# A decoder layer's first stage: keys stored by remainders of 16, a recurrence of one copy and eight links, and a step moved in its stream

## The chip, the cores and the metric

The kernel runs on one core of one Trainium2 chip. The metric is the device time in microseconds, median of several runs. The engines are named as in the trace: PE (matmuls; PEld its weight loads), DVE, ACT, POOL, and SP, which here only issues transfers.

## The reference

A decoder layer over 2048 tokens of 1024 features in float32. After an RMS norm, one input projection gives queries, keys and values for 8 attention heads of 64 features, and query, forget gate, input and output gate for 8 heads of a gated linear recurrence. Attention runs three times per head and the results are weighted by their softmax denominators:

```python
DILATED_CONFIGS = ((128, 1), (512, 4), (2048, 16))   # window, dilation
scores = einsum('bgnqhd,bgnkhd->bgnhqk', qb, kk) / sqrt(Dh)   # blocks of 128 queries, keys of this and the last block
scores = where(valid, scores - slope * (sub_dist * dilation), -inf)
```

With dilation d a block takes every d-th token: 128 queries, and the 128 keys of the block and those of the block before it (with dilation 16 there is only one block per remainder). The recurrence works on chunks of 32 tokens here, and on chunks of 64 in the kernel:

```python
log_f = log(lb + (1 - lb) * sigmoid(f_raw)); key = (1 - lb) * sigmoid(-f_raw); q = silu(q)
b = cumsum(log_f)                                     # within a chunk
A = where(causal, (q * exp(b)) @ (key * exp(-b)).T, 0)
dS = (key * exp(b_last - b)).T @ v;  S_next = exp(b_last) * S + dS
o = A @ v + (q * exp(b)) @ S
```

An output projection follows, then 32 experts in 4 groups, of which each token takes 2, and a last norm.

## The kernel before

**Stages.** Stage A (up to about 1134 us) computes projections, attention and recurrence for four pairs of heads. Then come output projection and router, and from about 1388 us the experts. Only stage A is changed; the later ones begin when it ends.

**Order of PE.** PE's instructions in stage A stand in an order written out by a planner (`Runner`, line 123). Work is cut in steps, each with a cost in ns and a list of steps that it follows with a delay (`Step(fn, cost, after)`). There are streams: H, the recurrence; G, weights; A, attention; F, projections. Within a stream the order is fixed; at each point the first stream whose next step is ready by the planner's clock goes on. The other engines' queues follow from that order and priorities: a step that is emitted later has, as a rule, its ACT, DVE and POOL instructions later. Each engine works its queue in order.

**Attention.** Queries and keys of a pair are held with the features on partitions, keys as high and low float16 halves (`qk_chunk`, drained from the accumulators by ACT in line 358 and by DVE in line 359). A block of scores (line 436) is four matmuls: two heads, two halves. The 128 queries are the weights that PE loads, the up to 256 keys stream past. `block_cols` takes both at steps of the dilation in tokens, 2 bytes each. After exponentials (ACT, line 453) and transposing transfers come the value matmuls (lines 471 and 473). The dilations run in the order 1, 16, 4. In the last one `combine` loads the results of the other two (tile `R`, line 506) and mixes them (POOL lines 529 and 531, DVE among them line 532).

**Recurrence.** Four token tiles of 128 make a quad, four quads a pair; each tile's projections are lines 567 to 569. Six steps follow for a quad: `gates` (lines 595 to 609, on ACT, DVE and POOL: logarithms, sigmoids, products), `decays` (line 615: sums over a chunk), `states` (line 643: the eight dS of a quad; ACT drains them in line 647; then a chain over eight chunks in which POOL scales the last state, line 658, and DVE adds dS, line 661), `turns` (transposes, line 672, drained by ACT in line 674), `within` (line 683, masked by DVE in line 684) and `outputs` (lines 693 and 697). The accumulators for these, named hg, have two buffers. The projections of quad q+2 come behind the outputs of quad q, since they share buffers.

## Time and profile before

| | us |
|---|---|
| median of 3 runs (2206.78 to 2219.48) | 2217.72 |
| the profiled execution | 2217.23 |
| its span, first to last instruction | 2215.3 |
| PE busy in the span | 1967.0 (89%) |
| DVE busy | 1493.8 (67%) |
| ACT busy | 1201.4 (54%) |
| POOL busy | 567.3 (26%) |

The mean granted clock of PE was 0.943 of full speed. The profile is of one execution; a group of instructions by line shows its busy time, the mean of one in ns, and the idle time of the engine just before them with what ended it. A name such as `hg<-Sp,qT` says which tile is written and which are read. In a timeline, `x4` is four instructions that follow one another; PE's instructions overlap, so what four cost is the distance between the start of theirs and the start of the next instruction, and not their duration.

### The profile page before, as it was taken

Reading aid. Unit: us, or ns where it says so; the run is one execution under the profiler, and the core shown is the slowest. Engines: PE = TensorE matmul, PEld = TensorE weight load, DVE = VectorE, ACT = ScalarE, POOL = GpSimd, SP = SyncE. Lnnn points to the kernel's source line nnn. Section 1 sums busy time; section 2 is a strip of 40 time slices with the busy share of each in tenths; the row PEclk is TensorE's granted clock in tenths of the full one; section 3 lists DMA queues with packets and bytes.
Section 4 is the critical chain, followed back from the end, with each engine's and each line's share of the span. In section 5 each row is a group of like instructions: output and inputs, shape, how many; then the busy total and the mean of one; then the engine's idle time right before and its main releaser. Section 6 shows DMA issues by size and latency. Waiting matters only on the chain. (4 is left out here: it accounts for less than half of the span.)

```text
span 2215.3 us, 39749 instructions
## 1 busy us (share of the span) xinstructions
PE 1967.0 (89%) x13753; PEld 1345.8 (61%) x13777; DVE 1493.8 (67%) x4121; ACT 1201.4 (54%) x2646; POOL 567.3 (26%) x620
## 2 busy tenths in 40 slices
PE   4998978999899998899888998699999999999981
PEld 4645565555655556455444445569999977766750
DVE  6657787767857777567887677756656656556525
ACT  6455653765547655566554343456556655555524
POOL 2303244123431335411431112212233222111110
PEclk9998988998999998999899998799999999999995
DMA  7333254532535324553578995799999999999857
GB/s 229 85 94 96 66 128 112 114 90 70 118 101 123 83 75 113 174 119 71 128 168 226 290 253 164 253 353 315 312 311 314 329 315 313 325 325 321 302 149 299
DMA packets 438896, 433.37 MB, mean 196 GB/s; under 512 B 242644, under 2 KB 325716, under 8 KB 438176
## 3 DMA queue, kind: packets, MB, share of 16 engines
q1 hardware_dynamic: 420464, 382.74, 56.7%
q0 software_dynamic: 14064, 46.46, 8.5%
q8 instruction: 109, 1.79, 0.3%
q10 hardware_dynamic: 4160, 1.58, 0.3%
q14 instruction: 99, 0.81, 0.1%
HBM read 305.30 MB, written 66.29 MB: 168 GB/s over the span
## 5 line engine op out<-in xcount | busy, mean ns | idle before, releaser
L1660 DVE TENSOR_TENSOR eL<-eraw,eH 128x1024 bf16<-128x1024 f32 x248 | 298.0, 1218 | 107.9 <-ACT eH L1654 97.0
L1654 ACT ACTIVATE eH<-eraw 128x1024 fp32r<-128x1024 f32 x252 | 258.4, 1053 | 123.8 <-PE acc L1745 48.8
L453 ACT ACTIVATE P<-S,orow,fqk 128x256 f32<-128x256 f32 (+1 forms) x384 | 195.0, 512 | 172.3 <-DVE orow L447 94.1
L567 PE MATMUL proj<-whh,x 128*128 128x512 f16 x512 | 202.4, 395 | 0.1
L568 PE MATMUL proj<-whl,x 128*128 128x512 f16 x512 | 200.1, 391 | 0.0
L569 PE MATMUL proj<-whh,x 128*128 128x512 f16 x512 | 199.5, 390 | 0.0
L1726 PE MATMUL acc<-xs,eH 128*128 128x352 f32 (+15 forms) x1216 | 195.2, 313 | 1.8 <-DVE xs L1704 1.8
L436 PE MATMUL S<-k,qs 128*128 128x256 f16 (+1 forms) x768 | 172.4, 355 | 13.9 <-ACT P L453 10.9
L1726 PEld LDWEIGHTS acc<-xs,eH 128*128 128x128 f32 x1216 | 176.2, 190 | 4.7 <-issue 2.2
L440 DVE CUSTOM_DVE_ANT_0 S<-S,bias 128x256 f32<-128x256 f32 (+1 forms) x384 | 141.4, 369 | 54.8 <-PE S L436 51.6
L456 DVE TENSOR_TENSOR Ps<-P,Ps 128x256 f16<-128x256 f32 (+1 forms) x192 | 129.7, 675 | 68.8 <-ACT Ps L455 67.2
L1828 POOL DMA_INDIRECT x2d<-yo,sidx x49 | 105.2, 2146 | 255.7 <-DVE yo L1803 95.8
L1776 PE MATMUL acc<-hs,eD 128*128 128x176 f32 (+15 forms) x1216 | 165.1, 295 | 4.9 <-DVE ts L1751 3.0
L1776 PEld LDWEIGHTS acc<-hs,eD 128*128 128x128 f32 x1216 | 161.1, 190 | 6.0 <-DVE ts L1751 3.9
L1687 POOL DMA_INDIRECT xg<-h2d,gidx x49 | 56.1, 1146 | 334.0 <-PE tr L1701 159.6
L436 PEld LDWEIGHTS <-qs 128*128 128x128 f16 x768 | 89.5, 123 | 69.3 <-issue 20.3
L260 POOL TENSOR_TENSOR wraw<-wraw,g 128x1024 f32<-128x1024 f32 x44 | 84.7, 1928 | 167.8 <-DMA wraw<-in_w_in_dram 134.5
L1744 PE MATMUL acc<-eH,xs 128*128 128x512 f32 x208 | 118.4, 569 | 0.0
L1788 PE MATMUL acc<-eD,hs 128*128 128x512 f32 x208 | 98.0, 609 | 21.2 <-ACT yo L1801 11.5
L386 PE MATMUL proj<-wh,x 128*128 128x128 f16 x512 | 96.5, 231 | 18.9 <-DVE V L394 18.9
L455 ACT ACTIVATE Ps<-P 128x256 f16<-128x256 f32 (+1 forms) x192 | 102.8, 536 | 7.6 <-DMA PT<-Ps 5.0
L658 POOL TENSOR_SCALAR sw<-Sp,hw 128x128 f32<-128x128 f32 x112 | 53.3, 476 | 196.5 <-DVE Sp L661 106.5
(396 smaller groups left out, 4891.6 us busy)
## 6 DMA issues: line engine op xcount, KB each, us to landing
eraw<-in_w_gate_dram SPq DMA_DIRECT2D x128, 512.0 KB, 7.1
eD<-in_w_down_dram SPq DMA_DIRECT2D x128, 512.0 KB, 6.4
eraw<-in_w_up_dram SPq DMA_DIRECT2D x124, 512.0 KB, 6.3
wraw<-in_w_in_dram SPq DMA_DIRECT2D x41, 512.0 KB, 4.1
od<-orow SPq DMA_DIRECT2D x64, 132.0 KB, 2.0
R<-od SPq DMA_DIRECT2D x64, 132.0 KB, 2.4
xt<-in_x_dram SPq DMA_DIRECT2D x16, 512.0 KB, 4.8
wraw<-in_w_out_dram SPq DMA_DIRECT2D x16, 512.0 KB, 4.1
```

What stands on the lines that cost most here:

```text
L436: nc.tensor.matmul(ps[:, h, :W], q, self.block_cols(D['k'][h][:, x], br, blk, True), start=(x == 0), stop=(x == 1))
L440: nc.vector.tensor_tensor_reduce(ps[:, h, :W], ps[:, h, :W], bias[:, 256 - W:256], 1.0, -3.0e38, OP.add, OP.max, mx[:, h:h + 1])
L453: nc.scalar.activation(P[:, h], ps[:, h, :W], AF.Exp, bias=nm[:, h:h + 1], scale=f[:, h:h + 1], accum_out=orow[:, 130 + h:131 + h])
L456: nc.vector.tensor_tensor(hv[:, 1], P, hv[:, 0], op=OP.subtract)
L567: nc.tensor.matmul(ps, self.XH[n // 4][:, k, ns], W['whh'][:, k, :], start=(k == 0), stop=False)
L568: nc.tensor.matmul(ps, self.XH[n // 4][:, k, ns], W['whl'][:, k, :], start=False, stop=False)
L569: nc.tensor.matmul(ps, self.XL[n // 4][:, k, ns], W['whh'][:, k, :], start=False, stop=(k == KT - 1))
L1654: nc.scalar.activation(H, raw, AF.Copy)
L1660: (nc.gpsimd if on_pool else nc.vector).tensor_sub(L, raw, H.bitcast(F32))
L1726: nc.tensor.matmul(gu[:, i, 0:2 * cap], w[:, o:o + 128], xs[:, k], start=(k == 0), stop=False, skip_group_check=True)
L1744: nc.tensor.matmul(gu[:, j], xs[:, k, 0], H[:, fs], start=(k == 0), stop=False)
L1776: nc.tensor.matmul(py[:, j, 0:cap], W['w_down', f][:, o:o + 128], hs[:, f], start=(f == 0), stop=(f == 3))
```

## The change

**Keys.** Each stretch of 512 tokens of the keys is stored by remainder of 16: 16 groups of 32 keys. `block_keys` then reads runs of 32 neighbouring keys for dilations 16 and 4, and runs of 8 for dilation 1. The drains read the accumulators at steps of 16 elements (64 bytes). Queries stay as they were. Since the keys of a block now come in another order, the values for dilation 1 are loaded again from memory in that order, those for dilation 4 too, and each dilation has its own table of distances, which SP loads.

**Recurrence.** dS is multiplied by the decays by POOL (two instructions), the chain is eight instructions on DVE over a compact tile `Sc`, and two ACT copies put the states in `Sp`. The transposed keys have their own tile `kT`. `R` has one buffer. States, turns and score products are split into two steps each, and their order is turns, states, products, outputs, with other costs and delays.

**Order.** The gates of a quad are put into the stream H five places from its end, which is ahead of the states (`s0`) of the quad before.

```diff
@@ -354,9 +356,13 @@
             a, b = slice(64 * h, 64 * h + 64), slice(64 - 64 * h, 128 - 64 * h)
             t = D["qk"[which]][h]
             hi, lo = (t[a, cs], t[b, cs]) if which == 0 else (t[a, 0, cs], t[a, 1, cs])
+            src = ps[a]
+            if which == 1:
+                src = src.rearrange("p (a r) -> p r a", r=16)
+                hi, lo = (x.rearrange("p (r a) -> p r a", r=16) for x in (hi, lo))
             sc = PSC / 2 if which == 0 and h == 0 else PSC
-            nc.scalar.activation(hi, ps[a], AF.Copy, scale=sc)
-            nc.vector.scalar_tensor_tensor(lo, ps[a], sc, hi, op0=OP.mult, op1=OP.subtract)
+            nc.scalar.activation(hi, src, AF.Copy, scale=sc)
+            nc.vector.scalar_tensor_tensor(lo, src, sc, hi, op0=OP.mult, op1=OP.subtract)
             if which == 1:
                 nc.gpsimd.dma_start(t[b, :, cs], t[a, :, cs])
 
@@ -389,38 +395,64 @@
...
-    def block_cols(self, t, br, blk, keys):
+    def block_queries(self, t, br, blk):
 
         dil = DIL[br]
         r, n = blk % dil, blk // dil
-        lo = n - 1 if keys and n else n
-        return t[:, r + lo * 128 * dil:r + (n + 1) * 128 * dil - dil + 1:dil]
+        return t[:, r + n * 128 * dil:r + (n + 1) * 128 * dil - dil + 1:dil]
+
+    def block_keys(self, t, br, blk):
+
+        r, n = blk % DIL[br], blk // DIL[br]
+        t = t.rearrange("p (g r a) -> p g r a", g=4, r=16)
+        if br == 3:
+            return t[:, :, r]
+        if br == 2:
+            return t.rearrange("p g (q c) a -> p c g q a", c=4)[:, r, max(n - 1, 0):n + 1]
+        cols = [t[:, m // 4, :, 8 * (m % 4):8 * (m % 4) + 8] for m in (n - 1, n) if m >= 0]
+        if len(cols) == 1:
+            return cols[0]
+        a, b = cols
+        return bass.AP(tensor=a.tensor, offset=a.offset, ap=[a.ap[0], [b.offset - a.offset, 2], *a.ap[1:]])
+
...
@@ -431,9 +463,9 @@
         f, bias = D['f'], D['bias', br]
         ps = self.psum([128, 2, 256], "S", 2)
         for h in range(2):
-            q = self.block_cols(D['q'][h], br, blk, False)
+            q = self.block_queries(D['q'][h], br, blk)
             for x in range(2):
-                nc.tensor.matmul(ps[:, h, :W], q, self.block_cols(D['k'][h][:, x], br, blk, True), start=(x == 0),
+                nc.tensor.matmul(ps[:, h, :W], q, self.block_keys(D['k'][h][:, x], br, blk), start=(x == 0),
                                  stop=(x == 1))
         mx = self.asm.tile([128, 2], F32, name="mx")
         for h in range(2):
@@ -499,7 +531,7 @@
...
-        R = self.ap_.tile([128, 2, 2, ROW], F32, name="R", bufs=2)
+        R = self.ap_.tile([128, 2, 2, ROW], F32, name="R", bufs=1)
@@ -633,55 +665,53 @@
             nc.vector.tensor_add(w, sv[:, :, 0], sv[:, :, 1])
             nc.scalar.activation(w, w, AF.Exp)
 
-        def states():
+        def states(ch):
             ek, v, w = L['sg'][:, :, 128:256], L['hq'][:, :, 384:512], L['w']
-            ds = []
-            for ch in range(2):
-                hs = slice(64 * ch, 64 * ch + 64)
-                pd = self.psum([128, 4, 128], "hg", 2)
-                for i in range(4):
-                    nc.tensor.matmul(pd[:, i, :], ek[hs, i, :], v[hs, i, :], start=True, stop=True)
-                d = hp.tile([128, 4, 64], F32, name=f"dS{ch}", bufs=1)
-                for h in range(2):
-                    hs = slice(64 * h, 64 * h + 64)
-                    nc.scalar.activation(d[hs], pd[hs, :, hs], AF.Copy)
-                ds.append(d)
-            sp = self.Sp
-
+            ds = L.setdefault('ds', [])
+            hs = slice(64 * ch, 64 * ch + 64)
+            pd = self.psum([128, 4, 128], "hg", 2)
+            for i in range(4):
+                nc.tensor.matmul(pd[:, i, :], ek[hs, i, :], v[hs, i, :], start=True, stop=True)
+            d = hp.tile([128, 4, 64], F32, name=f"dS{ch}", bufs=1)
+            for h in range(2):
+                hs = slice(64 * h, 64 * h + 64)
+                nc.scalar.activation(d[hs], pd[hs, :, hs], AF.Copy)
+            ds.append(d)
+            if ch == 0:
+                return
+
+            sc, sp = self.Sc, self.Sp
+            wv = w.rearrange("p (a b) -> p b a", b=2)
+            for ch, n, a in ((0, 4, wv[:, 1]), (1, 3, wv[:, 0, 1:4])):
+                nc.gpsimd.tensor_tensor(ds[ch][:, 0:n], ds[ch][:, 0:n], a[:, :, None].to_broadcast([128, n, 64]), op=OP.mult)
             if q == 0:
-                nc.gpsimd.memset(sp[:, 0], 0.0)
+                nc.vector.memset(sc[:, 0], 0.0)
             else:
-                nc.vector.tensor_scalar(sp[:, 0], sp[:, 8], w[:, 0:1], None, op0=OP.mult)
+                nc.vector.tensor_scalar(sc[:, 0], self.Send, w[:, 0:1], None, op0=OP.mult)
             for j in range(1, 8):
-                d = ds[(j - 1) % 2][:, (j - 1) // 2, :]
-                tmp = self.asm.tile([128, 128], F32, name="sw")
-                nc.gpsimd.tensor_scalar(tmp, sp[:, j - 1], w[:, j:j + 1], 1.0, op0=OP.mult, op1=OP.mult)
-                for h in range(2):
-                    hs = slice(64 * h, 64 * h + 64)
-                    nc.vector.scalar_tensor_tensor(sp[hs, j, hs], d[hs], w[hs, j:j + 1], tmp[hs, hs],
-                                                   op0=OP.mult, op1=OP.add)
+                nc.vector.scalar_tensor_tensor(sc[:, j], sc[:, j - 1], w[:, j:j + 1], ds[(j - 1) % 2][:, (j - 1) // 2],
+                                               op0=OP.mult, op1=OP.add)
             if q < 3:
-                for h in range(2):
-                    hs = slice(64 * h, 64 * h + 64)
-                    nc.gpsimd.tensor_tensor(sp[hs, 8, hs], sp[hs, 7, hs], ds[1][hs, 3], op=OP.add)
-
-        def turns():
-            for o, nm in ((128, "kT"), (0, "qT")):
-                pt = self.psum([128, 4, 128], "hg", 2)
-                for i in range(4):
-                    nc.tensor.transpose(pt[:, i, :], L['sg'][:, i, o:o + 128], c['ident'])
-                t = L[nm] = hp.tile([128, 4, 128], F32, name=("key" if nm == "kT" else nm), bufs=1)
-                nc.scalar.activation(t, pt, AF.Copy)
-
-        def within():
+                nc.vector.tensor_add(self.Send, sc[:, 7], ds[1][:, 3])
+            for h in range(2):
+                hs = slice(64 * h, 64 * h + 64)
+                nc.scalar.activation(sp[hs, :, hs], sc[hs], AF.Copy)
+
+        def turns(o, nm):
+            pt = self.psum([128, 4, 128], "hg", 2)
+            for i in range(4):
+                nc.tensor.transpose(pt[:, i, :], L['sg'][:, i, o:o + 128], c['ident'])
+            t = L[nm] = hp.tile([128, 4, 128], F32, name=nm, bufs=1)
+            nc.scalar.activation(t, pt, AF.Copy)
+
+        def within(h):
             qT, kT = L['qT'], L['kT']
             cm = c['causal'].bitcast(I32)[:, None, :].to_broadcast([128, 4, 128])
-            for h in range(2):
-                hs = slice(64 * h, 64 * h + 64)
-                pa = self.psum([128, 4, 128], "hg", 2)
-                for i in range(4):
-                    nc.tensor.matmul(pa[:, i, :], kT[hs, i, :], qT[hs, i, :], start=True, stop=True)
-                nc.vector.copy_predicated(self.Am[h], cm, pa)
+            hs = slice(64 * h, 64 * h + 64)
+            pa = self.psum([128, 4, 128], "hg", 2)
+            for i in range(4):
+                nc.tensor.matmul(pa[:, i, :], kT[hs, i, :], qT[hs, i, :], start=True, stop=True)
+            nc.vector.copy_predicated(self.Am[h], cm, pa)
 
         def outputs():
             hq, qT, sp = L['hq'], L['qT'], self.Sp
@@ -710,13 +740,17 @@
             nc.sync.dma_start(self.mix[q * 512:q * 512 + 512, 512 + 128 * p:640 + 128 * p]
                               .rearrange("(n p) c -> p n c", p=128), y)
 
+
         g = Step(gates, 0, [(ready, 1000)])
-        d = Step(decays, 1700, [(g, 14000)])
-        s = Step(states, 1700, [(d, 4000)])
-        t = Step(turns, 900, [(s, 1500)])
-        a = Step(within, 1700, [(t, 2800)])
-        o = Step(outputs, 3400, [(a, 2500), (s, 11000)])
-        return [g, d, s, t, a, o]
+        d = Step(decays, 1600, [(g, 20000)])
+        t0 = Step(lambda: turns(128, "kT"), 450, [(d, 6500)])
+        t1 = Step(lambda: turns(0, "qT"), 450, [(t0, 0)])
+        s0 = Step(lambda: states(0), 720, [(t0, 2500)])
+        s1 = Step(lambda: states(1), 720, [(s0, 0), (t1, 2500)])
+        a0 = Step(lambda: within(0), 720, [(t1, 3500), (s0, 2500)])
+        a1 = Step(lambda: within(1), 720, [(a0, 0), (s1, 2500)])
+        o = Step(outputs, 3700, [(a0, 6000), (a1, 5000), (s1, 9000)])
+        return [g, d, t0, t1, s0, s1, a0, a1, o]
 
     def phase_a(self, ctx, pairs=range(NPAIR)):
         self.last_pair = pairs[-1]
@@ -851,14 +893,14 @@
                 dep = [(st['q', g], 2000), (st['k', g], 5500)]
                 if i:
                     dep.append((S_[i - 1], 2300 if p == self.last_pair else 2500))
-                S_[i] = Step(lambda i=i: score(i), 430, dep)
+                S_[i] = Step(lambda i=i: score(i), 440 if blk >= DIL[br] else 240, dep)
                 A.append(S_[i])
             if i >= LAG:
                 j = i - LAG
-                dep = [(S_[j], 11000)]
+                dep = [(S_[j], 15500)]
                 if seq[j][0] == 1:
                     dep.append((st['v', 4 * (seq[j][1] // 4) + 3], 2500))
-                P_[j] = Step(lambda j=j: value(j), 330, dep)
+                P_[j] = Step(lambda j=j: value(j), 470 if seq[j][1] >= DIL[seq[j][0]] else 240, dep)
                 A.append(P_[j])
         out = {('quad', q): P_[2 * NT + 4 * q + 3] for q in range(4)}
         return dict(out, qk=S_[n - 1], v=P_[2 * NT - 1])
@@ -879,7 +921,10 @@
             if n % 4 == 3:
                 steps = self.quad_steps(p, q, hs, s)
                 last[q] = steps[-1]
-                H += steps
+
+                at = max(len(H) - 5, 0)
+                H[at:at] = steps[:1]
+                H += steps[1:]
         return last
 
 
```

The lines of the changed kernel are higher: 436 became 468, 471 and 473 became 503 and 505, 567 to 569 became 599 to 601, 595 to 609 became 627 to 641, 615 became 647, 643 became 674, 647 became 678, 672 became 703, 683 became 713, 693 and 697 became 723 and 727. The POOL product of dS is line 686, a link of the chain on DVE line 692, the ACT copies line 698.

**What moves on PE.** The second quad of the second pair, early in the attention's dilation 4, from the states to the outputs, with the change (line 601 is a projection, 674 states, 468 scores, 713 products of the recurrence, 503 and 505 values, 723 and 727 outputs):

```order
L601 MATMUL proj<-whh,x_123 128x512
L674 MATMUL hg<-hq,sg 128x128 x8
L503 LDWEIGHTS PT
L503 MATMUL O<-V,PT 128x128
...
L468 MATMUL S<-k_4238,qs_4198 128x128
L713 MATMUL hg<-qT,kT 128x128 x8
...
L505 MATMUL O<-V,PT 128x64
...
L468 LDWEIGHTS qs_4198
L468 MATMUL S<-k_4238,qs_4198 128x256
L723 MATMUL hg<-Sp,qT 64x128 x2
L727 MATMUL hg<-hq,Am_105 128x64
```

Between the states and the outputs stand three blocks of scores, three of values and the products 713, and no projection. The same quad before, from the states to the products (line 683):

```order
L569 MATMUL proj<-whh,x_122 128x512
L643 MATMUL hg<-hq,sg 128x128 x8
...
L473 MATMUL O<-V,PT 128x64
L567 LDWEIGHTS x_118
L567 MATMUL proj<-whh,x_118 128x512
...
L569 MATMUL proj<-whh,x_122 128x512
L672 MATMUL hg<-ct,sg 128x128 x8
...
L569 MATMUL proj<-whh,x_122 128x512
L683 MATMUL hg<-qT,key 128x128 x8
```

There projections (lines 567 to 569) stand between the steps, and more of them before the outputs.

**What moves on ACT.** The same quad with the change: 627 to 638 are gates of the next quad, 678 the drains of dS, 698 the first copy to `Sp`:

```order
L627 ACTIVATE key<-hq 128x512
L678 ACTIVATE dS_6094<-hg 64x256
L628 ACTIVATE hq<-key 128x4x128
L636 ACTIVATE sg<-hq 128x1024
...
L629 ACTIVATE hq<-hq 128x4x128
L637 ACTIVATE sg<-sg 128x1024
L678 ACTIVATE dS_6094<-hg 64x256
L638 ACTIVATE sg<-sg 128x1024
L678 ACTIVATE dS_6102<-hg 64x256
L633 ACTIVATE hq<-hq 128x4x128
L678 ACTIVATE dS_6102<-hg 64x256
...
L698 ACTIVATE Sp<-Sc 64x8x64
```

The gates stand among the drains of dS, 633 ahead of the last one. Before, 647 being the drain, only work of the attention and the copies of the transposes (674) stood there:

```order
L647 ACTIVATE dS_6070<-hg 64x256 x2
L647 ACTIVATE dS_6078<-hg 64x256
L516 ACTIVATE w<-w 128x12
L647 ACTIVATE dS_6078<-hg 64x256
L480 ACTIVATE otmp<-O 128x256
L453 ACTIVATE P,orow<-S,orow,fqk 128x128 x2
L674 ACTIVATE key<-hg 128x512
```

**What moves on POOL.** With the change the gates of the next quad (631, 632, 634) are ahead of the products of dS (686):

```order
L631 TENSOR_TENSOR hq<-hq,lb 128x4x128
L561 TENSOR_TENSOR R<-R,w 128x2x128 x2
L632 TENSOR_TENSOR hq<-hq,lb 128x4x128
L563 TENSOR_TENSOR R<-R 128x2x128
L634 TENSOR_TENSOR key<-key,lb 128x512
L686 TENSOR_TENSOR dS_6094<-dS_6094,hw 128x256
L686 TENSOR_TENSOR dS_6102<-dS_6102,hw 128x192
```

Before, the quad's own gates (599, 602, 600) are done ahead of its chain (658) and no other quad's stand there:

```order
L599 TENSOR_TENSOR hq<-hq,lb 128x4x128
L602 TENSOR_TENSOR key<-key,lb 128x512
L600 TENSOR_TENSOR hq<-hq,lb 128x4x128
L423 TENSOR_SCALAR bias<-cta,slope 128x256
L658 TENSOR_SCALAR sw<-Sp,hw 128x128 x3
```

Three gate operations have moved from one quad's place to the place ahead of another's products.

## Rows read from the trace of the kernel before

**Rows 1.** The page, part 1: busy time, share of the span, instructions

```profile
PE 1967.0 (89%) x13753; PEld 1345.8 (61%) x13777; DVE 1493.8 (67%) x4121; ACT 1201.4 (54%) x2646; POOL 567.3 (26%) x620
```

**Rows 2.** Windows of pair 1, dilations 16 and 4: stretch, length, engines, clock, DMA

```profile
438.00:502.00 64.00, 61.07 (x373) 35.77 (x372) 45.19 (x168) 41.78 (x122) 16.04 (x18) 1.00 0.39 90
502.00:584.00 82.00, 74.38 (x443) 42.99 (x442) 66.96 (x261) 45.20 (x133) 29.16 (x42) 0.90 0.35 81
```

**Rows 3.** Timeline of PE: start, duration, line, operation, operands

```profile
382.10 0.39 PE L436 MATMUL S<-k,qs 128*128 128x128 f16 x4
382.32 0.38 PE L348 MATMUL proj<-x,wh 128*128 128x512 f16 x1
...
401.01 0.60 PE L436 MATMUL S<-k,qs 128*128 128x256 f16 x4
401.44 0.38 PE L348 MATMUL proj<-x,wh 128*128 128x512 f16 x1
...
438.01 1.11 PE L436 MATMUL S<-k,qs 128*128 128x128 f16 x4
438.94 0.40 PE L567 MATMUL proj<-whh,x 128*128 128x512 f16 x1
...
541.28 1.08 PE L436 MATMUL S<-k,qs 128*128 128x256 f16 x4
542.18 0.24 PE L471 MATMUL O<-V,PT 128*128 128x128 f16 x1
```

**Rows 4.** Line L436, weight loads, dilations 1, 16, 4: minimum/median/maximum ns, first and last

```profile
L436 PEld LDWEIGHTS <-qs x63: 95/98/98, 382.1 to 434.7; 128*128 128x128 f16 x63
L436 PEld LDWEIGHTS <-qs x63: 143/148/179, 438.0 to 499.3; 128*128 128x128 f16 x63
L436 PEld LDWEIGHTS <-qs x64: 111/116/257, 502.4 to 583.4; 128*128 128x128 f16 x64
```

**Rows 5.** Groups by line, PE: busy, mean ns, then idle before and its releasers

```profile
L672 PE MATMUL hg<-ct,sg 128*128 128x128 f32 x128 | 20.8, 293 | 18.6 <-ACT dS L647 18.5
L615 PE MATMUL hg<-hq,cta 128*128 128x512 f32 x32 | 17.7, 635 | 8.8 <-ACT hq L601 8.8
L683 PE MATMUL hg<-qT,key 64*128 64x128 f32 x256 | 29.9, 302 | 7.2 <-ACT qT L674 7.2
L697 PE MATMUL hg<-hq,Am 128*128 128x64 f32 x256 | 49.5, 319 | 10.3 <-DVE Am L684 10.3
L693 PE MATMUL hg<-Sp,qT 128*64 128x128 f32 x256 | 31.3, 326 | 12.2 <-DVE Am L684 9.3 <-DVE den L521 2.9
L386 PE MATMUL proj<-wh,x 128*128 128x128 f16 x512 | 96.5, 231 | 18.9 <-DVE V L394 18.9
```

**Rows 6.** Timelines of ACT and POOL, the gates of one quad

```profile
448.01 0.63 ACT L595 ACTIVATE key<-hq 128x512 f32<-128x512 f32 x1
...
454.33 1.29 POOL L599 TENSOR_TENSOR hq<-hq,lb 128x512 f32<-128x512 f32 x1 [3.82 <-DVE orow L447]
457.25 1.71 POOL L600 TENSOR_TENSOR hq<-hq,lb 128x512 f32<-128x512 f32 x1
```

**Rows 7.** Groups by line, ACT and DVE: busy, mean ns, then idle before

```profile
L647 ACT ACTIVATE dS<-hg 64x256 f32<-64x256 f32 x64 | 24.0, 375 | 5.1 <-PE hg L643 4.2
L661 DVE SCALAR_TENSOR_TENSOR Sp<-dS,hw,sw 64x64 f32<-64x64 f32 x224 | 74.1, 331 | 29.7 <-POOL sw L658 23.9 <-ACT dS L647 2.2
L609 DVE TENSOR_TENSOR hq<-hq,sg 128x512 f32<-128x512 f32 x32 | 37.2, 1175 | 4.4 <-ACT sg L606 4.4
L684 DVE COPY_PREDICATED Am<-cta,hg 128x512 f32<-128x512 int32 x32 | 22.5, 724 | 0.3
```

**Rows 8.** Timeline of PE, the last quad: states, and first matmul of the outputs

```profile
1176.25 1.71 PE L643 MATMUL hg<-hq,sg 64*128 64x128 f32 x16
1187.08 0.44 PE L693 MATMUL hg<-Sp,qT 128*64 128x128 f32 x4 [2.19 <-DVE Am L684]
```

**Rows 9.** The page, part 6: one group; KB each, us to landing

```profile
R<-od SPq DMA_DIRECT2D x64, 132.0 KB, 2.4
```

More of the change, by code (lines that the diff above doesn't have):

```diff
@@ L73, in shape_tables @@
     parts['spare'] = np.stack([2048 + p, 2048 + 128 + p], 1).astype(f)
+    for br, tk in ((1, 16 * (tt % 8) + tt // 8), (2, 4 * (tt % 32) + tt // 32), (3, tt)):
+        parts[f'd{br}'] = dist(128 + tt, np.concatenate([tk, 128 + tk]), 1)
     off, cols = {}, 0
@@ L379, in v_tile @@
         if n == 0:
-            D['V', 1] = self.vp.tile([128, NT, 2, 128], F16, name="V", bufs=2)
+            D['V'] = self.vp.tile([128, NT, 2, 128], F16, name="V", bufs=2)
         if n % 4 == 0:
@@ L397, in v_tile, with load_v @@
                                 vs.rearrange("p n h c -> p n (h c)"))
-    def load_v(self, D, br):
+    def load_v(self, D, br, g=0):
         nc, vd = self.nc, D['vd']
-        V = D['V', br] = self.vp.tile([128, NT, 2, 128], F16, name="V", bufs=2)
+        if g == 0:
+            D['V', br] = self.vp.tile([128, NT, 2, 128], F16, name="V", bufs=2)
+        V = D['V', br]
         Vf = V.rearrange("p n h c -> p n (h c)")
         dil = DIL[br]
+        if br == 1:
+            for n in range(4 * g, 4 * g + 4):
+                src = bass.AP(tensor=vd.tensor, offset=vd.offset + n * 128 * 256,
+                              ap=[[256, 16], [16 * 256, 8], [1, 256]])
+                nc.sync.dma_start(Vf[:, n], src)
+            return
+        rows = [[4 * 256, 4], [16 * 256, 32]] if br == 2 else [[dil * 256, 128]]
@@ L405, in load_v @@
         for n in range(NT // dil):
[L406 to L407 removed]
+            src = bass.AP(tensor=vd.tensor, offset=vd.offset + n * 128 * dil * 256, ap=rows + [[1, dil * 256]])
             nc.sync.dma_start(Vf[:, n * dil:n * dil + dil, :].rearrange("p n c -> p (n c)"), src)
[L411 removed]
+    def block_queries(self, t, br, blk):
         dil = DIL[br]
@@ L744, in phase_a @@
             nc.scalar.dma_start(self.g1, self.aps['norm1_g'][0].rearrange("(t p) -> p t", p=128))
-            self.Sp = apool.tile([128, 9, 128], F32, name="Sp")
+            self.Sp = apool.tile([128, 8, 128], F32, name="Sp")
+            self.Send = apool.tile([128, 64], F32, name="Send")
             nc.vector.memset(self.Sp, 0.0)
@@ L769, in phase_a @@
                 self.ap_ = self.hp = pool("ap", 2)
+                self.Sc = self.hp.tile([128, 8, 64], F32, name="Sc", bufs=1)
                 self.asm = pool("asm", 2)
@@ L831, in score @@
             if i == 0:
+                if p == 0:
+                    self.bias_load(1)
                 self.bias_tile(D, p, br)
-            if blk == 8 and br != 2:
-                self.bias_tile(D, p, {1: 3, 3: 2}[br])
+            if br == 1 and blk % 4 == 0:
+                self.load_v(D, 1, blk // 4)
+            if blk == 8 and (br != 2 or p < self.last_pair):
+                self.bias_load({1: 3, 3: 2, 2: 1}[br])
+                if br != 2:
+                    self.bias_tile(D, p, {1: 3, 3: 2}[br])
             with self.tc.high_priority(offset=130):
@@ L1224, in route_setup @@
         _, off = shape_tables()
-        self.load_consts(rp, off['before'][0], self.aps['cst'].shape[1], "ctr")
+        self.load_consts(rp, off['before'][0], off['d1'][0], "ctr")
         self.gf = rp.tile([128, DM], F32, name="gf")
```

14 lines of the change are left out of this document (8 added, 6 removed).

## Prediction

> **What bounds the kernel now.** I read the page first: TensorE (PE) is busy for 89% of the span, DVE for 67% and ACT for 54% [rows 1], so PE sets the time and another engine counts only where PE waits for it. Then the stage windows of the second head pair [rows 2]: with dilation 16 PE is idle for under 3 us of 64, with dilation 4 for 7.6 of 82, where the granted clock is 0.90 as well. So before the expert layer the kernel is a stream of matmuls with small gaps, and a saved matmul is saved time as long as the gaps stay small. Everything behind the attention stage starts when it ends; I move it as a block. Then the rows of the score matmuls with the matmul behind each [rows 3], and the groups of lines in which PE waits for the recurrence [rows 5].
>
> **Scores.** Four matmuls make one block of scores; their cost is the distance from the first to the next instruction. For dilation 1, keys side by side: 401.01 to 401.44, 0.43 us for 256 columns each, and 382.10 to 382.32, 0.22 us for 128. For dilation 16, keys 32 bytes apart: 438.01 to 438.94, 0.93 us for only 128 columns, 233 ns a matmul. For dilation 4, 8 bytes apart: 541.28 to 542.18, 0.90 us for 256 [all rows 3]. The change makes runs of 32 keys of the last two, and runs of 8 of the first. The queries, which PE loads as weights, stay strided: that load takes 143 to 179 ns with dilation 16 and 95 to 98 with dilation 1 [rows 4]. With dilation 1 a load of 95 ns stands beside a step of 55 ns, so some 40 ns of the record are no hindrance; for dilation 16 that leaves a step of about 100 ns (estimate), between 55 (loads hidden) and 143 (not hidden). Four pairs with 16 blocks per dilation: dilation 16 64 x (0.93 - 0.40) = 34 us; dilation 4 48 blocks of two key blocks x (0.90 - 0.43) = 23, and 16 short ones at about 0.2 = 3. **-60 us**. Ends: -72 with steps of 55 ns; -31 with steps of 143 (64 x 0.36 = 23, and 23) less 15 us if runs of 8 keys cost dilation 1 half of what the 8-byte step costs (64 x 0.24).
>
> [...]
>
> **Recurrence waits that go.** The ping-pong of POOL and DVE over eight states (L658, L661) becomes two POOL multiplications, eight DVE operations and two ACT copies, and transposes, states and score products are separate steps with other work between them. In the trace PE waits 18.6 us before the transposes L672, 8.8 before L615, 7.2 before L683, 12.2 and 10.3 before the outputs L693 and L697 [rows 5]. I let all of it go: **-57 us**. The POOL and DVE time saved lies beside PE and counts nothing by itself.
>
> **The wait that is added.** The next quad's gates now stand in the recurrence's stream ahead of this quad's states. Gates need the projections of their quad complete, the streams run in order, and the projections of the quad after it wait for this quad's outputs. So when PE comes to the states, no projection is left that it may run before the outputs. The order of PE shows it: before, the states and the outputs had 10 to 15 us of other matmuls between them; now in 9 of the 16 quads only two to three blocks of scores, four to eight value matmuls with each, and eight L713, about 3.5 us (scores 0.43 each [rows 3], L713 as L683, 29.9 us for 256 [rows 5]). In 6 more there are 9.6 to 10.1 us; the last quad has what it had.
>
> What must happen between states and outputs is now a longer queue. The orders of ACT and POOL put the gates in front: on ACT L627, L628, L636, L629, L637, L638 and L633 stand before the last drain of dS (L678), and L633 waits for POOL's L632; POOL multiplies dS (L686) only behind L632. In the trace the same gates took from 448.01 (L595) to the end of L600 at 458.96, 10.9 us, 3.8 of which was POOL waiting for something else [rows 6]. Started about 1.6 us after the states' first matmul, when the last projection tile is drained, POOL is done at 8.7 to 12.6 us. Then L633 and the two dS drains, 0.6 + 2 x 0.38 [rows 7]; POOL's L686, about 0.7; the chain on DVE, eight times 0.33 with, between its links, two gate products of 1.18 and two masked copies of 0.72 [rows 7], 5 to 7 us; two ACT copies with an exponential between them, about 1.5. Sum 17 to 23 us; I take **20**. The nearest row of before is the last quad, where nothing else was in the queue: 1176.25 to 1187.08, 10.8 us [rows 8]. That is the lower bound.
>
> PE's wait: 9 x (20 - 3.5) + 6 x (20 - 9.8) = 149 + 61 = **+210 us**; at 17 us 165, at 23 us 255, at 10.8 us 72.
>
> **Small terms.** The drains of the keys (ACT L358, DVE L359) now read the accumulators at 64-byte steps. No row shows such a read; a drain of 64x256 with unit steps takes 375 ns [rows 7], so I call one of 64x512 0.75 us and a doubling 0.75 us more; 32 on ACT bound it at 0 to +24 us. [...] With one buffer for R instead of two, each of 32 combinations may see the landing of its loads, 2.4 us [rows 9]: 0 to +77, but this delays ACT, DVE and POOL; PE has other blocks. V is loaded again in another order for dilation 1, with 16 more transfers per pair on SP, whose loads lie early; the distance tables are loaded in place of one held. I take +10 for all of these. Waits of the V projections for their drains (18.9 us before L386 [rows 5]) halve, since DVE empties its queue while PE waits: -9. [...]
>
> **Sum.** -60 - 57 + 210 + 10 - 9 = +94 us on the profiled execution's 2217.2, which lies 0.5 below the median shown: **2310 us**. Its own range takes 17 to 23 us for the queue: 2265 to 2355, and with R's and the scores' ends a little beyond.
>
> **Rivals.**
> *Faster: the queue is short.* If the gates don't hold the drains up (their first operations done before the states, POOL free at once), states to outputs take what the last quad took, 10.8 us [rows 8], and the waits are 72: -60 - 57 + 72 + 1 = -44, **2173 us**; with steps of 55 ns and a better clock 2140. The point is 13.8 us from states to outputs, where 15 x 13.8 - 90 equals the 116 saved. For it: PE waits 10.3 to 12.2 us in all there now, and the new chain has one handover per link where the old one had two. Against: the order of the queues, and gates that took 10.9 us in the trace. Chance 0.3.
> *No difference.* 12.4 to 15.2 us from states to outputs give 2195 to 2240: gates half in front. Chance 0.15. (About 1%, 22 us, is what a measurement of this kernel can tell from no change.)
> *The 8-byte step was not what cost.* If dilation 4 is slow for its queries and not for its keys, its 26 us stay: **2336 us**. [...] Against: the loads of the queries take 111 to 116 ns there, hardly more than the 95 to 98 of dilation 1 [rows 4], while the block takes twice as long [rows 3]. Chance 0.05.
> *R's single buffer or the key drains become a bound.* Dilation 4 stretches by the landing, 32 x 2.4 = 77 us: up to **2385 us**. Against: SP has little to do there. Chance 0.05.
>
> **How the numbers follow.** The forecast has 0.45. Slower by over 1% are the forecast and the last two rivals: 0.55. Same 0.15, faster 0.3. The range leaves out the tail of the faster rival below 2150 and what lies above 2365: 2150 to 2365.
>
> **What would show it.** Score blocks of dilation 4 at 0.43 us and of dilation 16 near 0.40. PE idle before L723 and L727 of well over 100 us in sum, ended by ACT's Sp (L698), in 9 stretches of about 16 us with PE slices at 7 or below in pairs 1 to 4; states to outputs 17 to 23 us. No idle time before L703. Wrong would be: outputs that start 14 us or less behind the states; an R load that ends DVE's waits by more than 20 us; a key drain much over 0.75 us.

## The result, and the profile after

The changed kernel takes 2401.23 us (median of 4 runs, 2398.65 to 2403.49), the kernel before beside it 2215.18. The ratio is 1.084, with a 95% interval of 1.081 to 1.088: slower by 186 us. The prediction was 2310, from 2150 to 2365: right in sign, short by half.

The page after, parts 1 and 2 (busy time of each engine; then PE's busy share and its granted clock in tenths, in 40 slices):

```profile
PE 1965.7 (82%) x13777; PEld 1363.9 (57%) x13777; DVE 1442.5 (60%) x4025; ACT 1223.9 (51%) x2678; POOL 526.5 (22%) x512
...
PE   5997877777788787678777888969999999999991
...
PEclk9996889877888888788777989969999999999995
```

PE is as long busy as before (1965.7 against 1967.0 us [rows 1]), though the scores are cheaper: in the first 23 slices it runs at a lower clock and stands more. Stage A as one window, from the first scores to the last outputs, first of the kernel before, then after (stretch, length, then busy time of PE, PEld, DVE, ACT, POOL, granted clock, DMA):

```profile
121.00:1191.50 1070.50, 964.02 (x6707) 586.21 (x6706) 781.90 (x2653) 623.62 (x1659) 329.81 (x413) 0.93 0.46 110
```

```profile
118.00:1369.50 1251.50, 959.28 (x6689) 604.22 (x6686) 727.89 (x2536) 643.10 (x1685) 287.93 (x306) 0.83 0.41 96
```

All but 4 us of the loss lies there: what follows the last outputs takes 1024 us before and 1028 after. (The 1134 us given for the end of this stage ahead of the prediction is where the output projection begins; the recurrence of the last quads goes on to 1191.5 beside it.) I take the stage apart in three, for this and every run below. Idle is the sum of the idle times before PE's instructions. Half clock is half of the time at the lower level in which PE was not idle: the granted clock is 0.50 there, as from 471.7 to 492.2 us in the changed kernel, where a projection matmul steps by 0.426 us (five from 486.68 to 488.81); at 1.00 right after it steps by 0.215 (six from 492.32 to 493.61). The rest is work at full clock.

| stage A, us | length | work | idle | half clock |
|---|---|---|---|---|
| before | 1070.5 | 905 | 106 | 59 |
| after | 1251.5 | 830 | 292 | 129 |
| difference | +181 | -75 | +186 | +70 |

**Work.** Score blocks after: dilation 1, dilation 16, dilation 4 (timeline of PE, the next instruction's start ends a block), then the weight loads of dilation 16:

```profile
405.70 0.60 PE L468 MATMUL S<-k,qs 128*128 128x256 f16 x4 [0.26 <-ACT P L485]
406.13 0.38 PE L350 MATMUL proj<-x,wh 128*128 128x512 f16 x1
...
512.05 0.44 PE L468 MATMUL S<-k,qs 128*128 128x128 f16 x4
512.33 0.38 PE L599 MATMUL proj<-whh,x 128*128 128x512 f16 x1
...
632.98 0.60 PE L468 MATMUL S<-k,qs 128*128 128x256 f16 x4
633.42 0.38 PE L599 MATMUL proj<-whh,x 128*128 128x512 f16 x1
...
L468 PEld LDWEIGHTS <-qs x63: 141/153/177, 489.4 to 569.0; 128*128 128x128 f16 x63
```

Dilation 16 went from 0.93 to 0.28 us a block, dilation 4 from 0.90 to 0.44 [rows 3]; dilation 1, with runs of 8 keys, stayed at 0.43.

**Idle.** The waits of PE after (us in total, times, longest):

```profile
PE hg L713 <- ACT dS L678: 140.3, 20, 22.0
PE S L468 <- DMA k<-k: 34.0, 12, 7.7
PE hg L723 <- ACT Sp L698: 31.0, 10, 5.8
PE hg L269 <- ACT dS L678: 23.0, 2, 12.0
```

L269 is a small matmul for the weights that takes its accumulator from the same two buffers. Before, L683, which is L713 now, waited 7.2 us [rows 5], for something else. One of the waits in whole, on PE, ACT and POOL (start, duration, and in brackets the idle time and its releaser):

```profile
465.34 1.71 PE L674 MATMUL hg<-hq,sg 64*128 64x128 f32 x16
...
468.85 0.38 PE L601 MATMUL proj<-whh,x 128*128 128x512 f16 x1
482.23 3.09 PE L713 MATMUL hg<-qT,kT 64*128 64x128 f32 x16 [13.00 <-ACT dS L678]
```

```profile
470.32 0.63 ACT L627 ACTIVATE key<-hq 128x512 f32<-128x512 f32 x1
...
477.15 0.37 ACT L678 ACTIVATE dS<-hg 64x256 f32<-64x256 f32 x1
477.41 1.05 ACT L638 ACTIVATE sg<-sg 128x1024 f32<-128x1024 f32 x1
481.15 0.63 ACT L633 ACTIVATE hq<-hq 128x512 f32<-128x512 f32 x1 [2.69 <-POOL hq L632]
481.79 1.17 ACT L678 ACTIVATE dS<-hg 64x256 f32<-64x256 f32 x3
```

```profile
476.58 1.65 POOL L631 TENSOR_TENSOR hq<-hq,lb 128x512 f32<-128x512 f32 x1 [2.63 <-DVE key L630]
478.20 1.26 POOL L634 TENSOR_TENSOR key<-key,lb 128x512 f32<-128x512 f32 x1
479.42 1.70 POOL L632 TENSOR_TENSOR hq<-hq,lb 128x512 f32<-128x512 f32 x1
```

PE has finished the states at 467 and needs an accumulator buffer, of which there are two, both full of dS. ACT begins the next quad's gates at 470.3, drains a part at 477.2, waits for POOL with L633, and frees the buffer after 481.8.

**The key copy.** When a stretch of keys is drained, POOL issues a transfer that copies both its halves to the other 64 partitions, and the scores wait for it. For the last keys of pair 1 the projections on PE end at 428.0; the scores that wait, on PE, and the drains, on ACT:

```profile
435.81 0.59 PE L468 MATMUL S<-k,qs 128*128 128x256 f16 x2 [5.89 <-DMA k<-k]
438.06 0.37 PE L468 MATMUL S<-k,qs 128*128 128x256 f16 x1 [1.66 <-DMA k<-k]
```

```profile
430.93 0.57 ACT L364 ACTIVATE k<-proj 64x512 f16<-64x512 f32 x1
432.37 0.59 ACT L364 ACTIVATE k<-proj 64x512 f16<-64x512 f32 x1 [0.87 <-DVE k L365]
```

The planner allows 5.5 us from projection to scores; here it was 10. The drain itself, with its reads at 64-byte steps, takes 0.57 to 0.59 us; the mean of 32 is 588 ns, and 587 in the kernel before.

### The profile page after: what moved, and what is told of

The parts are those of the page before. It is cut to its first block, busy times and chain, and to the rows that moved or that the text cites. A ratio compares the mean times of both kernels' runs of the same rounds, so it can differ in the third digit from the quotient of the medians.

```text
span 2397.9 us, 39602 instructions
## 1 busy us (share of the span) xinstructions
PE 1965.7 (82%) x13777; PEld 1363.9 (57%) x13777; DVE 1442.5 (60%) x4025; ACT 1223.9 (51%) x2678; POOL 526.5 (22%) x512
## 5 line engine op out<-in xcount | busy, mean ns | idle before, releaser
L599 PE MATMUL proj<-whh,x 128*128 128x512 f16 x512 | 205.9, 402 | 13.2 <-ACT hq L606 13.2
L600 PE MATMUL proj<-whl,x 128*128 128x512 f16 x512 | 205.9, 402 | 0.0
L601 PE MATMUL proj<-whh,x 128*128 128x512 f16 x512 | 204.2, 399 | 0.0
L488 DVE TENSOR_TENSOR Ps<-P,Ps 128x256 f16<-128x256 f32 (+1 forms) x192 | 118.2, 616 | 137.3 <-ACT Ps L487 136.2
L713 PE MATMUL hg<-qT,kT 64*128 64x128 f32 x256 | 53.7, 419 | 141.4 <-ACT dS L678 140.3
L468 PE MATMUL S<-k,qs 128*128 128x256 f16 (+1 forms) x768 | 116.0, 279 | 42.7 <-DMA k<-k 34.0
L713 PEld LDWEIGHTS hg<-qT,kT 64*128 64x128 f32 x256 | 47.2, 308 | 147.6 <-ACT dS L678 145.3
L350 PE MATMUL proj<-x,wh 128*128 128x512 f16 x256 | 102.0, 398 | 14.9 <-DVE V L400 14.1
```

Of the source, the lines that this page charges most:

```text
L468: nc.tensor.matmul(ps[:, h, :W], q, self.block_keys(D['k'][h][:, x], br, blk), start=(x == 0), stop=(x == 1))
L488: nc.vector.tensor_tensor(hv[:, 1], P, hv[:, 0], op=OP.subtract)
L599: nc.tensor.matmul(ps, self.XH[n // 4][:, k, ns], W['whh'][:, k, :], start=(k == 0), stop=False)
L600: nc.tensor.matmul(ps, self.XH[n // 4][:, k, ns], W['whl'][:, k, :], start=False, stop=False)
L601: nc.tensor.matmul(ps, self.XL[n // 4][:, k, ns], W['whh'][:, k, :], start=False, stop=(k == KT - 1))
```

## The experiments

Theory Q: the gates, queued ahead of the drains on ACT and POOL, are the cost. Theory P: the place itself is, since PE has nothing else to run there.

**e1**, the order on PE untouched, the states' work on the other engines put ahead:

```diff
+        def early(ch):
+            with self.tc.high_priority(offset=400):
+                states(ch)
-        s0 = Step(lambda: states(0), 720, [(t0, 2500)])
-        s1 = Step(lambda: states(1), 720, [(s0, 0), (t1, 2500)])
+        s0 = Step(lambda: early(0), 720, [(t0, 2500)])
+        s1 = Step(lambda: early(1), 720, [(s0, 0), (t1, 2500)])
```

> The changed kernel with one edit: the states step (the drains of dS, POOL's products, the chain on DVE, the copies to Sp) gets a priority, so that on ACT, POOL and DVE it stands ahead of most of the next quad's gates. PE's order is the same, word for word. Theory Q (the queue: what costs is that the gates stand ahead of the drains on ACT and POOL): PE's wait before L713 falls from 140 us to under 30, that before L723 may rise to 30 to 80, since 9 quads have 3.5 us of other work against a chain of about 10; idle time falls by some 100 us, the half-clock cost by 30, time about 2270 (2230 to 2310). Theory P (the place: PE has no projection to run between states and outputs, whoever is in front): the wait only changes its name from L713 to L723, their sum stays over 140 us, time 2360 or more.

Measured 2304.04 us, ratio 1.039 (1.035 to 1.043): 97 us less than the change. Its waits:

```profile
PE S L468 <- DMA k<-k: 40.2, 12, 8.3
PE hg L723 <- ACT Sp L698: 28.1, 11, 3.8
...
PE hg L713 <- ACT dS L678: 16.7, 13, 4.4
```

L713's wait fell from 140 to 17 and L723's did not take its place (31 before this edit, 28 with it). That is Q, shown, for these 97 us. Half clock stayed at 129 us, though idle fell by 100 (292 to 192). Stage A of e1, in the form of the two windows above:

```profile
118.00:1273.90 1155.90, 964.05 (x6684) 603.82 (x6684) 721.74 (x2534) 643.03 (x1684) 284.30 (x306) 0.86 0.45 104
```

**e2**, the gates in order:

```diff
-                at = max(len(H) - 5, 0)
-                H[at:at] = steps[:1]
-                H += steps[1:]
+                H += steps
```

> The changed kernel with the gates back at the end of their stream (H += steps), all else as changed. In its order on PE most quads still have only 3 to 4 us of other work between states and outputs, 6 have about 10. Theory Q: without the next quad's gates in the queues the drains follow the states at once; waits before L713 and L723 together 40 to 80 us, time 2130 to 2200, faster than the kernel before. Theory P: the place without projections is as it was, so the waits stay at over 140 us, time 2330 or more.

2262.89, ratio 1.022 (1.019 to 1.025): 138 us less than the change, and still slower than before. Neither number was met. The waits:

```profile
PE hg L723 <- ACT Sp L698: 45.8, 11, 7.6
PE S L468 <- ACT P L485: 26.0, 15, 5.5
PE hg L674 <- ACT kT L705: 24.8, 9, 7.3
```

L713's is 10 us now. Something else in the change costs as well, which the two parts alone should show.

**e3**, the kernel before with the new key layout, values and tables, and two R buffers; **e4**, the kernel before with the new recurrence, its steps with their delays and one R buffer, gates in order. The edits are two parts of the change's diff; in both the planner keeps its old figures for the attention.

> The kernel before with the keys' layout, the values loaded again and the distance tables of the change; recurrence, order, costs and two R buffers as before. If the scores' saving is the 72 us that the score rows of the two traces give (dilation 16 from 233 to 64 ns a matmul, dilation 4 from 229 to 109) and PE stays the bound: 2145 (2130 to 2160). Rival: ACT and DVE, which had cover beneath the slow scores, become what PE waits for and half of it is given back: 2180 to 2200.

> The kernel before with the changed recurrence (POOL products, eight links on DVE, copies, own kT, split steps, one R buffer) and its gates in order; keys and the planner's costs of the attention as before. Theory Q: the recurrence itself does no harm; the 57 us of waits of before go, and 30 to 70 come before L713 and L723 in quads with little other work: 2190 to 2240. Theory P: quads whose states and outputs have 3.4 to 5.6 us between them wait as in the changed kernel: 2300 or more.

e3: 2230.81, ratio 1.007 (1.005 to 1.009). e4: 2288.15, ratio 1.033 (1.029 to 1.037). **The scores' gain is gone even with nothing else changed.** Stage A of e3: work 841 us (64 less), idle 163 (56 more), half clock 76 (17 more). The stretch of pair 1's dilation 16 in e3, to hold against [rows 2]:

```profile
435.00:500.00 65.00, 54.47 (x376) 31.76 (x373) 45.55 (x168) 42.18 (x123) 17.24 (x19) 0.95 0.50 92
```

PE has 6.6 us less to do and the stretch is 1 us longer; what grew is the wait of the values for their transposed probabilities, from 5.2 to 27.3 us in all, and that of the scores for the exponentials, from 10.9 to 18.6. The kernel before, then e3:

```profile
PE S L436 <- ACT P L453: 10.9, 11, 2.8
...
PE O L471 <- DMA PT<-Ps: 5.2, 7, 1.2
...
PE S L436 <- DMA k<-k: 2.9, 3, 1.6
```

```profile
PE O L503 <- DMA PT<-Ps: 27.3, 18, 4.7
...
PE S L468 <- ACT P L485: 18.6, 20, 2.8
```

e4 has 151 us of idle time and 88 of half clock; 69 us of the idle time stand before the outputs, for Sp. With the rearranged steps PE has, in nine of the 16 quads, only 4 to 8 us of other work between states and outputs.

Two theories for e3. L: the distances in PE's order, counted in PE's work, became too short. E: the other engines pace the attention.

**e5**, e3 with the change's figures for the planner (`score` 440 or 240, `value` 470 or 240, `(S_[j], 15500)`); **e6**, e3 with less on DVE, the low halves of the probabilities being left out (POOL sets them to zero):

```diff
-        nc.vector.tensor_tensor(hv[:, 1], P, hv[:, 0], op=OP.subtract)
+        nc.gpsimd.memset(hv[:, 1], 0.0)
```

> Keys alone (e3: PE has 66 us less work in stage A, but 57 us more idle time and 20 us more of the half clock, so 2231) with the planner's attention figures of the change: scores 440 or 240 ns, values 470 or 240, 15500 ns from a block's scores to its values. Theory L (the lags: the order of PE puts values, transposes and outputs at distances counted in PE time; with shorter scores the same distances pass before ACT, DVE and the transposing transfers are done): the waits for PT (27 us) fall under 8, those for dS, Am and qT stay, 2195 to 2215. Theory E (ACT and DVE are near their capacity in the attention, PE must wait for them whatever the order): 2225 to 2240.

> Keys alone (e3) with 130 us of DVE's work taken out of stage A: the low halves of the probabilities (line 488, 192 instructions of 0.675 us on DVE) are not computed but set to zero by POOL, a part of the computation that this run leaves out. Theory E (DVE's capacity): the 57 us of idle time that e3 had gained come down by half or more, 2170 to 2200. Theory L (distances in the order, not capacity): the chain of a block gets 0.7 us shorter and little else, 2210 to 2230.

e5: 2280.87, ratio 1.028 (1.024 to 1.032); waits for PT are no longer among its largest, but those for the key copy are 36.9 us, for the gates 32.7, for the masked products 29.0. The planner's new figures alone cost 50 us. e6: 2206.11, 0.995 (0.993 to 0.997), 25 us under e3. So what DVE does in the attention counts, be it as load on DVE or as a link in a block's chain; this run changes both. It did not give back the half of the idle time that E wanted (163 to 151, and half clock 76 to 67).

**e7**, e2 with the step delays of before (gates to decays 14000, decays to transposes 4000, products and states to outputs 2500 and 11000); **e8**, e3 with `bufs=1` for R.

> The changed kernel with its gates in order (e2, 2263) and the delays of before for the quad's steps (gates to decays 14000 instead of 20000, decays to transposes 4000 instead of 6500, products to outputs 2500, states to outputs 11000). In the order of PE the quads then have 5 to 12 us of other work between states and outputs instead of 3 to 4 in most. If the missing filler is what is left of the loss (theory P for this part): the waits before L723 (46 us) fall to 20, the clock follows, 2200 to 2225. If it is the two accumulator buffers that transposes, states and products share in their new order (waits before L674 of 25 us, L713 of 10): 2245 to 2270.

> Keys alone (e3, 2231) with one buffer for R instead of two. The rival of the prediction (each of 32 combinations sees its loads, 2.4 us): up to 2300. If R's loads hide behind other work: 2226 to 2240.

e7: 2257.24, 1.018 (1.014 to 1.022), no gain on e2 to speak of. Its wait for Sp fell from 46 to 7 us, but the scores wait 38.0 us for exponentials and 36.7 for the key copy. e8: 2247.53, 1.014 (1.010 to 1.018): the single R buffer costs 17 us, which the prediction had at nothing to 77.

**e9**, e3 with the new chain (POOL products, `Sc`, ACT copies) in the six old steps; **e10**, the same chain in the kernel before:

```diff
-                tmp = self.asm.tile([128, 128], F32, name="sw")
-                nc.gpsimd.tensor_scalar(tmp, sp[:, j - 1], w[:, j:j + 1], 1.0, op0=OP.mult, op1=OP.mult)
...
+                nc.vector.scalar_tensor_tensor(sc[:, j], sc[:, j - 1], w[:, j:j + 1], ds[(j - 1) % 2][:, (j - 1) // 2],
+                                               op0=OP.mult, op1=OP.add)
```

> Keys alone (e3, 2231) with the new chain (two POOL products, eight links on DVE, two ACT copies) in the place of the old one, in the old six steps, their old order and delays; PE's order is that of e3. Against the old chain it takes some 30 us of DVE's and 30 us of POOL's time away and 14 handovers per quad. Theory E (DVE and ACT are what PE waits for in stage A): part of the 57 us of idle time goes, 2190 to 2215, a little under the kernel before. If the chain is off PE's path in the old order, since 10 us of other matmuls lie over it: 2225 to 2235.

> The kernel before with the new chain alone, in the old steps; keys as before, two R buffers. Theory E: with PE's work at 905 us there are only 106 us of idle time to win, 15 to 30 of it: 2185 to 2205. If the chain is covered: 2212 to 2222.

e9: **2193.06**, 0.989 (0.987 to 0.992), the fastest of all and faster than both kernels. e10: 2196.88, 0.992 (0.989 to 0.994). The chain alone is worth 20 us, with 38 on top of e3. The keys add 4 us to it, inside the intervals. In stage A e10 has 4 us less idle time than the kernel before, and 14 less half clock (59 to 45); e9 has 9 and 16 less than e3. By these traces, one of each kernel, most of the chain's gain comes through the clock and not through waits, and why is open. Lines of e9 for the chain, to hold against L661 [rows 7]:

```profile
L690 DVE SCALAR_TENSOR_TENSOR Sc<-Sc,hw,dS 128x64 f32<-128x64 f32 x112 | 37.8, 337 | 13.1 <-POOL dS L684 11.9
...
L696 ACT ACTIVATE Sp<-Sc 64x512 f32<-64x512 f32 x32 | 20.0, 626 | 2.6 <-DVE Sc L690 2.2
```

**e11**, e7 with a longer delay; **e13**, the same number alone in the changed kernel:

```diff
-                dep = [(st['q', g], 2000), (st['k', g], 5500)]
+                dep = [(st['q', g], 2000), (st['k', g], 10000)]
```

> e7 (the changed kernel, gates in order, short delays, 2257) with the planned delay from a key projection to its scores at 10000 ns instead of 5500. In the trace of the change the last key projection ends at 427.8 us and the copy of the low half lands at 438.1, 10.3 us later. If the planner's 5.5 us are what makes PE stand before the scores of dilation 1 (37 us in e7, 34 in the change, 3 before): these fall under 12 and the time to 2215 to 2235. If the same time is then lost to the exponentials (38 us in e7): 2245 to 2260.

> The changed kernel (2401) with one number changed: 10000 ns instead of 5500 from a key projection to its scores in the planner. Theory K (PE stands before the scores of dilation 1 for the key's drains and copy, 10 us on the chip): the 34 us of waits for k fall under 12 and some clock comes back, 2350 to 2370. Rival: the time saved there is only spent in the next wait for the drains of dS, whose queue is the pace: 2385 to 2405.

e11: 2204.97, 0.995 (0.992 to 0.997), 52 us under e7 and a little under the kernel before. e13: 2365.32, 1.068 (1.066 to 1.070), 36 us under the change:

```profile
PE hg L713 <- ACT dS L678: 110.7, 19, 14.4
PE hg L723 <- ACT Sp L698: 47.0, 13, 5.8
...
PE S L468 <- DMA k<-k: 12.1, 6, 3.8
```

**e12**, matmuls whose result is thrown away, behind the states of 12 quads of the changed kernel:

```diff
+        self.fillw = W['whh']
...
+            if q < 3:
+                ps = self.psum([128, 512], "proj", 2)
+                for i in range(32):
+                    nc.tensor.matmul(ps, self.XH[q][:, 0, 0:128], self.fillw[:, 0, :], start=True, stop=True)
```

> The changed kernel (2401) with 32 matmuls of 512 columns, whose result is thrown away, behind the states of 12 of the 16 quads: 7 us of work for PE in the place where it waits before L713, 83 us in all. Nothing is left out of the computation. If the waits are fixed by ACT's queue, as theory Q has it, the filler lies inside them and costs nothing: the wait before L713 falls from 140 to about 70. If the half clock follows from PE standing still, its cost (129 us against 59 before) comes down by 20 to 40: 2360 to 2390. If it comes from something else, the time stays at 2400; if the filler adds to the waits, 2450 to 2485.

2397.98, 1.083 (1.079 to 1.086). Work in stage A rose by 86 us and idle fell by 82, to no effect on the time: the wait is set elsewhere, as Q has it. The wait of the products for dS fell from 140 to 45 us, and that of the scores for the exponentials rose from 7 to 48. The half clock's cost fell by 5 us only; that it would go with the standing still was wrong. Stage A of e12:

```profile
118.80:1369.40 1250.60, 1040.19 (x7074) 634.38 (x7073) 729.40 (x2530) 644.75 (x1684) 293.46 (x306) 0.86 0.41 96
```

**e14**, e9 with `LAG = 4`; **e15**, e14 with the 10000 of e13; **e16**, e9, and **e17**, e11, with the weight loads (`wraw`, line 261) issued by POOL instead of SP.

> Keys and chain (e9, 2193) with LAG = 4 instead of 3: the values of a block follow its scores four blocks later in PE's order instead of three (median distance 13.5 us of PE's work instead of 11.5). Theory L (the distance in the order is what became too short): the waits for PT (34 us) fall under 12, 2160 to 2180. Theory E (ACT, DVE and the transposing transfers pace the blocks of dilation 16 at some 4 us each whatever the order): PT's waits turn into waits of the scores for the exponentials (16 us now), 2188 to 2200.

> e14 with the planner's 10000 ns from a key projection to its scores. If both distances count: 2150 to 2175, under e14 by 5 to 10, for e9 still has 6 us of waits for k. If e14 gains nothing, this neither: 2185 to 2200.

> Keys and chain (e9, 2193) with the loads of the projection weights (line 261) issued by POOL instead of SP, so that no transposing transfer stands behind one that waits for its buffer. Theory H (head of the line on SP): of the 34 us of waits for PT 12 to 20 go, 2170 to 2185. Theory E (the pace of ACT and DVE in the attention): the waits for PT stay over 25, 2188 to 2200; POOL's time on issuing can make it worse, up to 2210.

> e11 (the change with gates in order, short delays and the longer key delay, 2205) with the same loads issued by POOL. PT's waits are 6 us there, so theory H gives little: 2198 to 2206. By theory E the same, or slower where POOL holds up the gates: 2200 to 2215.

None gained: 2208.16 (0.998, 0.996 to 1.000), 2233.55 (1.008, 1.006 to 1.010), 2217.61 (1.000, 0.998 to 1.002), 2239.12 (1.010, 1.007 to 1.013). In e14 the wait for PT fell from 34 to 22, and those for the copies of the transposes rose from 11 to 23; in e16 PT's was 39. That speaks against L as a remedy and against H, the blocked SP queue, as the cause of the waits for PT; as e16 also gives POOL the issuing, it is no clean measure of H. In e15 the longer key delay, which helped the changed order, brought waits for the key copy of 48 us: such a number is good for one order.

## Why the prediction was right in sign and short in size

- **Scores, -60.** Measured -75 of work in the whole change, -64 with the keys alone (e3) and -7 with the recurrence alone (e4). The end with hidden loads was nearly reached: 70 ns a matmul of dilation 16 beside weight loads of 141 to 177 ns. Keys were the cost; the rival by which the 8-byte step was not is refuted: with the queries as they were, a block of dilation 4 took 0.90 us with 8-byte steps and 0.44 with runs of 32.
- **The added wait, +210 against -57 and -9.** The cause held, and the sum nearly. Idle time of PE between the states' first matmul and the outputs was 40 us before and is 198 after; the states-to-outputs time has a median of 20.7 us over the 16 quads, where I had taken 20. It is e1 and e2 that show the cause. That the sum came so near 210 is in part luck: in the nine quads with little other work the idle time is 109 us where I had 149, and in the six with more it is 87 where I had 61, for there the outputs come 21 to 36 us behind the states, not 20. Where it stands was wrong: I had put it before L723 and L727 for Sp, and it stands mostly before L713, one step earlier, for the accumulator buffers that the same drains free. While it waits there PE does not run what stands behind L713 (13.0 us idle ahead of 482.23 in the wait shown above), and in the six quads only about 2 of the 9.8 us of other work that I had subtracted stand ahead of it. I had these two buffers in view when describing the kernel and not when pricing the queue. In the 20 us, the 0.7 for L686 and the 1.5 for the copies to Sp were estimates that no row of before shows; in the wait shown above two L686 take 0.62 and 0.52 us (at 482.26 and 483.04), and a copy (L698) takes 0.627 in the changed kernel (median of 32).
- **The clock, 0.** This is the step that failed most: +70 us. The forecast's sum gives it nothing and adds 150 us of standing still, which came in pieces of up to 22. The granted clock of the stage fell from 0.93 to 0.83. After the wait shown above it is at the lower level from 471.7 to 492.2, 10 us into PE's next work. What exactly governs it stays open: with e1 idle fell by 100 us and its cost did not, and filling waits (e12) moved it by 5. The time at the lower level did fall, from 437 us to 328 in e1 and 345 in e12, but PE's work within it hardly did: 258, 259 and 248 us. The faster rival's 2140 has some 21 us in it for a better clock (2173 less 12 for steps of 55 ns is 2161), and no run shows that term: the new chain alone took 14 us off the half clock (e10), the whole change added 70.
- **Small terms, +10.** The key copy was not in the sum: 34 us of wait after, 2.9 before; e13 puts 36 us on it with what follows. The new layout alone does not bring it (6.1 us in e3), the planner's new figures with it do (36.9 in e5), though not in every order (7.5 in e2). Those figures are a part of the change that had no term at all; on e3 they cost 50 us (e5). The key drains' reads cost nothing (588 against 587 ns), and a drain of this size takes less than the 750 ns that I had put down for it. R's single buffer cost 17 us (e8).
- **Sum.** -75 + 158 between states and outputs + 31 for the key copy - 3 elsewhere + 70 = 181, of 182.6 by which the spans differ. Against the +94 of the forecast the clock is 70 higher, idle time 32 (186 where the terms gave 210 - 57 - 9 + 10 = 154), and work 15 lower.
- **What neither the forecast nor its rivals said.** Even without the added wait the scores' gain would not have come: e3. The first paragraph of the prediction argued that with small gaps a saved matmul is saved time. DVE and ACT were busy for 55% to 82% of the time in [rows 2]; that the gaps were small because PE was slow enough for these two fits e3, but is argued and not shown. That less work on DVE, or less handing over between DVE and POOL, shortens the time is shown (25 us in e6 and 38 in e9, both against e3, and 20 in e10 against before); how much each engine has in the rest is open.

## What to carry to other kernels

Before crediting time to the busiest engine, ask what the others need per block at its new pace: 64 us off PE came to nothing, and 20 came from shortening a chain on DVE and POOL that PE hardly seemed to wait for. A step put earlier in a hand-written order puts its work on the other engines earlier too: look at what it is then ahead of in each queue, and at the buffers that the delayed work frees. Delays in such an order are made for one set of costs.

## What was not expected of the hardware

The weight loads of strided queries have records of 141 to 177 ns, yet the matmuls with them step at 70 ns. In the block at 512.05 the four loads start at 512.03, 512.07, 512.14 and 512.21, so the record of one overlaps that of the next as well as the matmuls, and its length is not what a load costs here. Reading accumulators at 64-byte steps costs ACT 1 ns of 588 in these drains, and DVE none of 688. And PE's lower clock outlasts a wait, the one shown above by 10 us (482.23 to 492.2): of the 437 us that stage A of the changed kernel spends at the lower level, 258 are work.
